# A decoder layer's down projection gets weight buffers of its own, and its weights are prepared three steps ahead

## The chip, the cores and the metric

The kernel runs on one core of one Trainium2 chip. Its time is the device time of one execution in microseconds. The engines of the core work side by side, each on its own queue of instructions, in order: PE (TensorE, matmuls and transposes), DVE (VectorE), ACT (ScalarE), POOL (GpSimd, here mainly a queue that issues DMAs) and SP (SyncE, a queue that issues DMAs). An instruction that waits for a semaphore holds everything behind it on its engine.

## The reference

One layer of a decoder, 512 tokens of width 2048, all in fp32: a modulation from c, an RMS norm, two attention mixers (one sparse with an indexer, one latent), a gated merge, and a feed-forward part with a causal convolution of width 3. The part around the change is the last line:

```python
h = rms_norm(x, g_ffn[l]) * (1.0 + sc_f) + sh_f
x = x + gt_f * conv_ffn(h, w_up[l], w_conv[l], b_conv[l], w_down[l])

def conv_ffn(h, w_up, w_conv, b_conv, w_down):
    u = h @ w_up                              # 2048 -> 2 * 5632
    conv = b_conv + sum(w_conv[j] * up[:, j:j + S] for j in range(3))   # up: u padded in front
    gate, val = split(conv)
    return (silu(gate) * val) @ w_down        # 5632 -> 2048
```

(Cut from the reference, with the loop over the convolution's taps written as a sum.)

## The kernel before, in words

**Precision.** fp32 products are made of three matmuls: each operand is split into a high part (`Copy` to fp32r on ACT) and a low part (the difference, on DVE), and high x high, high x low and low x high are accumulated (lines 1065 to 1067). So every weight tile costs one ACT and one DVE operation of its width before PE can use it; so does every activation tile (`split`, lines 113 to 115; the weights' halves are made by the same two lines).

**Seven products.** The gate, up and down projections go through `seven` (line 919). It multiplies a 2 x 2 block of weights with a 2 x 2 block of activations (the columns halved, 256 tokens each) in seven products of half-size blocks instead of eight. One `Pair` is a pair of 128-wide output columns, and has seven **steps**, in the order p1, p7, p6, p2, p5, p4, p3. Each step has a preparation (load blocks of weights, add or subtract them on DVE in `comb`, line 965, and make the halves in `hilo`), K x 3 matmuls of 256 columns, and an eviction from PSUM (e1, e7, e6 and e3 on ACT, line 969 or 971; e2, e5 and e4 on DVE, line 975 or 977). The first steps of a pair write one half of a bank pair each, and a later step of the same pair writes that bank again, so that it waits for the eviction of the step two before it.

**How far ahead.** The main loop (lines 1053 to 1070) prepares step q + 2 before it issues the matmuls of step q: AHEAD is 2. The weight buffers are five raw ones of 1104 columns, used in rotation through `rawq`, and three pairs of high and low (lines 81 to 91). All stages of the kernel use these. In most of the up projection some blocks lie in slots instead.

**The stages around the change.** The up projection is 40 pairs of K = 8 (280 steps, 24 matmuls and weight blocks of 1024 columns each). Each pair ends in a convolution, silu and product, and `f_out` writes the result f and the sums of it that the down projection needs to HBM, from POOL's queue. The down projection follows in the same list of steps: the 22 row pairs of f are cut in four **chunks** of `DH` = 6, 6, 5, 5, and each chunk goes over all eight pairs of output columns, 56 steps of K = 6 (18 matmuls, 768 columns) or K = 5 (15 matmuls, 640 columns). The results of the first three chunks are added to x1 in HBM by an accumulating DMA on POOL's queue (line 1526); the last chunk reads x1 back, adds it (line 1523) and writes the output.

**The activations of a chunk.** Each of the seven products of a chunk has its own operand, a "kind" of three tiles (two row pairs each, the last one half full where K = 5), which a chunk uses in all its eight pairs. `load_set` loads one kind of f from HBM into slots, on SP's queue, where the weight loads go too (line 1459). `split_set` splits a kind into high and low slots. `ahead` (line 1477) is called after each step; `left` is the number of steps until the chunk begins. It splits a whole kind every fourth step for four of the seven kinds, and one kind at every step from eight steps before the chunk on, as long as `2 * n + spare` slots are free. In the last seven steps of a chunk the kinds that are not needed any more are given back (line 1541).

**Slots.** 81 tiles of 128 x 512 fp32, handed out first in, first out (`get`, `put`). A slot that was given back may still be read by a DMA or an engine; who writes it next waits for that.

**Order.** The program is recorded in the order of the Python code, and a scheduler then orders each engine's instructions by priority and by its own estimate of times. So a split or a load may stand earlier on its engine than the code has it.

Of the kernel before, what the change touches and what calls it, by code (L numbers as in the profile page):

```python
# [10 lines left out]
F32 = mybir.dt.float32  # L11
# [20 lines left out]
def trunk_layer_kernel(  # L32
# [17 lines left out]
    PEU=((2, 5, 8, 11, 14),) * 2 + ((),) * 6,  # L50
    DH=(6, 6, 5, 5),
):
# [37 lines left out]

    rawq = deque(raw_b)

    def wtile(src, k0, kg, c0, n, pri=PRI, more=None):
        i = cnt["wt"] % NH
# [823 lines left out]

    def seven(work, pairs_of_banks, hook=None):
        def pair_steps(n, p):  # L920
# [34 lines left out]
            def hilo(t):  # L955
                i = cnt["wt"] % NH
# [15 lines left out]

            def plus(o, b, g, x):
                if g is not None:
                    V.scalar_tensor_tensor(o, b, g, x, op0=ALU.mult, op1=ALU.add)
                else:
                    V.tensor_tensor(o, b, x, ALU.add)  # L977

# [40 lines left out]
            def e1():  # L1019
                E["s"] = get()  # L1020
                copy(E["s"][:, :HT], X, g1)

            def e7():
                copy(E["s"][:, HT:], Y, g2)

            def e6():
                E["s6"] = get()
                copy(E["s6"][:, :HT], X, g2)

            def e2():  # L1030
                E["u1"] = get()
                plus(E["u1"][:, :HT], Z, g1, E["s"][:, :HT])

            def e5():
                E["u2"] = get()
                plus(E["u2"][:, HT:], X, g2, E["s"][:, HT:])
                put(E["s"])

            def e4():
                plus(E["u2"][:, :HT], Y, g2, E["s6"][:, :HT])  # L1040
                put(E["s6"])

# [7 lines left out]
        steps = [st + (p.K,) for n, p in enumerate(work) for st in pair_steps(n, p)]  # L1050
        AHEAD = 2
        ready = {}
        for q in range(len(steps) + AHEAD):
            if q < len(steps):
                ready[q] = steps[q][0]()
            if q < AHEAD:
                continue
            _, o, r, ev, first, K = steps[q - AHEAD]
            wh, wl = ready.pop(q - AHEAD)
            assert len(r) == K  # L1060
            for k in range(K):
                ks = slice(k * P, (k + 1) * P)
                rh, rl = r[k]
                last = k == K - 1
                PE.matmul(o, wh[:, ks], rh, start=first and k == 0, stop=False, skip_group_check=True)  # L1065
                PE.matmul(o, wh[:, ks], rl, start=False, stop=False, skip_group_check=True)  # L1066
                PE.matmul(o, wl[:, ks], rh, start=False, stop=last, skip_group_check=True)  # L1067
            ev()
            if hook:
                hook(q - AHEAD, len(steps))  # L1070

# [41 lines left out]
    seven([Pair(rs, lambda blk, i=i: w_gs[i, blk], gate_out(i)) for i in range((31 - G0) // 2)],  # L1113
          ((MM[0], MM[1]), (MM[2], MM[3])), gate_hook)
    for t in h[KH:] + [x for ts in h_sums for x in ts]:
        put(*t)
# [344 lines left out]

    def split_set():
        c, n, ts = coming.popleft()
        for i, t in enumerate(ts):
            hi, lo = getr(), getr()
            w = min(T, (DH[c] - 2 * i) * HT)
            split(hi[:, :w], lo[:, :w], t[:, :w])
            put(t)
            held_by[c][n] += [hi, lo]
            ops[c][n] += [(hi[:, o:o + HT], lo[:, o:o + HT]) for o in range(0, w, HT)]  # L1470

    def need(c):
        return (DH[c] + 1) // 2

    made = [0]

    def ahead(left, last):

        c = (coming or todo or [(9,)])[0][0]
        if c > last or left > 50:  # L1480
            return
        n, spare = need(c), 8 if c else 6
        if coming and coming[0][0] <= c and len(free) >= 2 * n + spare and (left <= 8 or left % 4 == 0 and made[0] < 4):
            made[0] = (made[0] + 1) % 7
            split_set()
        while todo and todo[0][0] <= c and len(coming) < (3 if c or len(free) > 15 else 1) and len(free) >= n + spare:
            load_set()


# [16 lines left out]
    work = [Pair(rs, lambda blk, i=i: w_ups[i, blk], ffn_out(i), slots=i < NF_ - 10) for i in range(NF_ - 4)]  # L1506
    n_up = len(work) * 7

# [23 lines left out]

    work += [down_pair(c, j) for c in range(len(DH)) for j in range(KD // 2)]

    def hook(q, n):
        if q < n_up:
            up_hook(q, n_up)
            return
        c, r = divmod(q - n_up, 56)
# [61 lines left out]
```

## Time and profile before

| | us |
|---|---|
| three runs, median | 2716.6 |
| lowest, highest | 2716.36, 2725.06 |
| profiled execution, as timed | 2718.77 |
| its span, first to last instruction | 2716.3 |
| mean granted TensorE clock | 0.99 |

All times of single instructions come from the profiled execution. The rows of windows give, for a stretch of the span, the time in which each engine was busy and the number of its instructions, then the granted TensorE clock, the mean busy share of the 16 DMA engines, and what they moved in GB/s. The rows of waits give who waited for whom: us in total, how often, the longest. In a row of a group stand line, engine, operation, what it writes and reads, count, busy time and mean duration in ns, then the idle time just before and what ended most of it. Names are those of the program without numbers: `raw`, `whi` and `wlo` are the weight buffers, `slot` a slot, `bank` a PSUM bank, `f` and `x` buffers in HBM, `in_w_down` the weights of the down projection.

The down projection's matmuls begin at about 2222 us of the span; the three changes of chunk are at about 2359, 2492 and 2608 us, and the last matmul ends at 2712 us.

### The profile page before, as it was taken

How to read it: one execution, taken by the hardware profiler on the slowest of the kernel's cores; microseconds unless marked ns; L12 is line 12 of the kernel's file. 1: busy time of each engine (PE TensorE's matmuls, PEld its weight loads, DVE VectorE, ACT ScalarE, POOL GpSimd, SP SyncE). 2: the span in 40 equal slices, each digit the busy share in tenths (PEclk: the TensorE clock that was granted, in tenths of full speed). 3: DMA queues.
4: the chain of work that ended last, by engine and by line, in shares of the span. 5: the costliest groups of instructions: out<-in, count | busy, mean ns of one | idle time of the engine just before them, and what ended most of it. 6: DMA issues, size and time to landing. Idle time of an engine off the chain costs nothing. (4 is left out here: it accounts for less than half of the span.)

```text
span 2716.3 us, 45517 instructions
## 1 busy us (share of the span) xinstructions
PE 2620.4 (96%) x17200; PEld 2351.7 (87%) x17200; DVE 2184.6 (80%) x3669; ACT 1285.3 (47%) x2069; POOL 270.5 (10%) x495
## 2 busy tenths in 40 slices
PE   6999999998999999999999999999999989898999
PEld 5777687778997767788789999999999989898989
DVE  7877966688878667983778989989889897777778
ACT  4333434334444455332545555555555464545554
POOL 1001011110032222110100000000000001011110
PEclk8999899999999999999999999999999999999999
DMA  9943136664585578962333333433433466766574
GB/s 343 341 153 98 34 110 213 197 214 156 190 269 164 161 255 288 323 238 93 132 114 124 134 137 113 147 120 114 148 120 128 140 205 154 187 141 173 137 206 125
DMA packets 236241, 464.33 MB, mean 171 GB/s; under 512 B 24331, under 2 KB 85413, under 8 KB 236021
## 3 DMA queue, kind: packets, MB, share of 16 engines
q1 hardware_dynamic: 199348, 368.79, 42.5%
q0 software_dynamic: 36640, 92.63, 11.7%
q8 instruction: 134, 2.20, 0.3%
q14 instruction: 87, 0.70, 0.1%
q10 hardware_dynamic: 32, 0.01, 0.0%
HBM read 397.11 MB, written 64.23 MB: 170 GB/s over the span
## 5 line engine op out<-in xcount | busy, mean ns | idle before, releaser
L1065 PE MATMUL bank<-slot,whi 128*128 128x256 f32 x3920 | 1109.9, 283 | 49.4 <-ACT slot L969 17.0
L1067 PE MATMUL bank<-slot,wlo 128*128 128x256 f32 x3920 | 1101.6, 282 | 8.3 <-DVE wlo L115 8.2
L1066 PE MATMUL bank<-slot,whi 128*128 128x256 f32 x3920 | 1104.4, 282 | 0.4 <-DVE slot L115 0.4
L1065 PEld LDWEIGHTS bank<-slot,whi 128*128 128x128 f32 x3920 | 743.4, 190 | 62.4 <-ACT slot L969 22.2
L1067 PEld LDWEIGHTS bank<-slot,wlo 128*128 128x128 f32 x3920 | 739.9, 189 | 10.8 <-DVE wlo L115 10.3
L1066 PEld LDWEIGHTS bank<-slot,whi 128*128 128x128 f32 x3920 | 741.7, 189 | 0.8 <-DVE slot L115 0.6
L114 ACT ACTIVATE whi<-raw 128x1024 fp32r<-128x1024 f32 (+2 forms) x458 | 424.6, 928 | 500.1 <-PE bank L1066 385.5
L115 DVE TENSOR_TENSOR wlo<-raw,whi 128x1024 fp32r<-128x1024 f32 (+2 forms) x458 | 482.1, 1056 | 61.7 <-ACT whi L114 59.6
L106 ACT ACTIVATE whi<-raw 128x1024 fp32r<-128x1024 f32 (+4 forms) x182 | 187.3, 1032 | 396.0 <-PE bank L120 201.8
L107 DVE TENSOR_TENSOR wlo<-raw,whi 128x1024 fp32r<-128x1024 f32 (+4 forms) x182 | 215.7, 1186 | 146.4 <-ACT whi L106 146.0
L965 DVE TENSOR_TENSOR raw<-raw,raw 128x1024 f32<-128x1024 f32 (+2 forms) x252 | 264.8, 1051 | 61.8 <-DMA raw<-in_w_down 33.3
L119 PE MATMUL bank<-wlo,slot 128*128 128x512 f32 (+2 forms) x768 | 297.4, 388 | 0.9 <-DVE wlo L107 0.9
L118 PE MATMUL bank<-whi,slot 128*128 128x512 f32 (+2 forms) x768 | 290.1, 391 | 4.7 <-ACT slot L385 4.3
L120 PE MATMUL bank<-whi,slot 128*128 128x512 f32 (+2 forms) x768 | 293.3, 385 | 0.0
L118 PE MATMUL bank<-slot,whi 128*128 128x512 f32 (+1 forms) x656 | 261.2, 405 | 3.3 <-ACT slot L1346 2.3
L119 PE MATMUL bank<-slot,whi 128*128 128x512 f32 (+1 forms) x656 | 263.1, 402 | 0.7 <-DVE slot L687 0.7
L120 PE MATMUL bank<-slot,wlo 128*128 128x512 f32 (+1 forms) x656 | 257.5, 401 | 0.0
L118 PEld LDWEIGHTS bank<-whi,slot 128*128 128x128 f32 x768 | 145.9, 190 | 36.1 <-ACT slot L385 4.3
L723 DVE SCALAR_TENSOR_TENSOR slot<-slot,c_act,slot 128x512 f32<-128x512 f32 x203 | 148.9, 745 | 33.9 <-DMA slot<-in_w_ada 32.8
L119 PEld LDWEIGHTS bank<-wlo,slot 128*128 128x128 f32 x768 | 146.2, 190 | 30.0 <-DVE wlo L107 1.4
L120 PEld LDWEIGHTS bank<-whi,slot 128*128 128x128 f32 x768 | 144.6, 188 | 29.0 <-issue 0.5
L114 ACT ACTIVATE whi<-slot 128x512 fp32r<-128x512 f32 x204 | 127.0, 630 | 79.4 <-PE bank L1066 63.8
(292 smaller groups left out, 3004.6 us busy)
## 6 DMA issues: line engine op xcount, KB each, us to landing
slot<-in_w_ada SPq DMA_DIRECT2D x344, 256.0 KB, 5.7
raw<-in_w_ups SPq DMA_DIRECT2D x126, 512.0 KB, 4.4
raw<-in_w_in SPq DMA_DIRECT2D x50, 512.0 KB, 3.6
raw<-in_w_down SPq DMA_DIRECT2D x64, 384.0 KB, 3.1
raw<-in_w_down SPq DMA_DIRECT2D x64, 320.0 KB, 3.4
slot<-f SPq DMA_DIRECT2D x154, 128.0 KB, 3.3
slot<-in_w_ups SPq DMA_DIRECT2D x68, 256.0 KB, 2.6
f<-slot POOLq DMA_DIRECT2D x66, 256.0 KB, 5.2
```

Source lines behind the costliest of these rows:

```text
L106: A.activation(hi, raw[:, :w], AF.Copy)
L107: V.tensor_tensor(lo, raw[:, :w], r32(hi), ALU.subtract)
L114: A.activation(dst_hi, src, AF.Copy)
L115: V.tensor_tensor(dst_lo, src, r32(dst_hi), ALU.subtract)
L118: PE.matmul(o, lh, rh, start=first, stop=False)
L119: PE.matmul(o, lh, rl, start=False, stop=False)
L120: PE.matmul(o, ll, rh, start=False, stop=last)
L723: V.scalar_tensor_tensor(acc, ts[i], c_act[:, k:k + 1], acc, op0=ALU.mult, op1=ALU.add)
L965: V.tensor_tensor(part(o, x, y), part(a, x, y), part(b, x, y), op)
L1065: PE.matmul(o, wh[:, ks], rh, start=first and k == 0, stop=False, skip_group_check=True)
L1066: PE.matmul(o, wh[:, ks], rl, start=False, stop=False, skip_group_check=True)
L1067: PE.matmul(o, wl[:, ks], rh, start=False, stop=last, skip_group_check=True)
```

## The change

- The weight buffers live in a pool of their own. When the last matmuls of the up projection have been issued in the code (`turn`), the pool is closed and opened anew at the same place, with seven raw buffers and four pairs of high and low, of 768 columns: 15 x 768 columns instead of 11 x 1104. A buffer of the new pool that overlaps one of the old pool waits for the old one's last use.
- `seven` returns two functions, `start` (the first AHEAD preparations) and `run`. The down projection is a list of its own with AHEAD = 3. The gate and up projections keep 2.
- The evictions add in place: e1 writes its half straight into `u1` and e7 and e6 into `u2`; e2, e5 and e4 add to them. The two helper slots of a pair are gone, and `u1` and `u2` are held from the first evictions on.
- The chunks are `DH` = 5, 6, 6, 5, and the packed weights follow.
- `split_tile` splits one tile instead of a kind, every third step from 54 steps before the chunk on, at every step from eight before, and a second one where the rest would not be done in time. It needs `2 + spare` free slots, and loading a kind needs its tiles and `spare`; `spare` is 12 (was 8) for all chunks but the first (6).

The diff, without the changes of the calls of `seven` for the gate projection, the packing and the renaming of `NH`:

```diff
-    NR, NH = 5, 3
-    WB = 1104
-    raw_b = [pool.tile([P, WB], F32, name=f"raw{i}") for i in range(NR)]
-    hi_b = [pool.tile([P, WB], F32R, name=f"whi{i}") for i in range(NH)]
-    lo_b = [pool.tile([P, WB], F32R, name=f"wlo{i}") for i in range(NH)]
+    wpool = ExitStack()
+    hi_b, lo_b, rawq = [], [], deque()
+    def weight_bufs(nr, nh, w):
+        wpool.close()
+        wp = wpool.enter_context(tc.tile_pool(name=f"w{w}", bufs=1))
+        rawq.clear()
+        rawq.extend([wp.tile([P, w], F32, name=f"raw{w}_{i}") for i in range(nr)])
+        hi_b[:] = [wp.tile([P, w], F32R, name=f"whi{w}_{i}") for i in range(nh)]
+        lo_b[:] = [wp.tile([P, w], F32R, name=f"wlo{w}_{i}") for i in range(nh)]
+    weight_bufs(5, 3, 1104)
...
-            def plus(o, b, g, x):
+            def plus(o, b, g):
                 if g is not None:
-                    V.scalar_tensor_tensor(o, b, g, x, op0=ALU.mult, op1=ALU.add)
+                    V.scalar_tensor_tensor(o, b, g, o, op0=ALU.mult, op1=ALU.add)
...
             def e1():
-                E["s"] = get()
-                copy(E["s"][:, :HT], X, g1)
+                E["u1"] = get()
+                copy(E["u1"][:, :HT], X, g1)
             def e7():
-                copy(E["s"][:, HT:], Y, g2)
+                E["u2"] = get()
+                copy(E["u2"][:, HT:], Y, g2)
             def e6():
-                E["s6"] = get()
-                copy(E["s6"][:, :HT], X, g2)
+                copy(E["u2"][:, :HT], X, g2)
             def e2():
-                E["u1"] = get()
-                plus(E["u1"][:, :HT], Z, g1, E["s"][:, :HT])
+                plus(E["u1"][:, :HT], Z, g1)
...
-        AHEAD = 2
-        for q in range(len(steps) + AHEAD):
+        def prepare(q):
             if q < len(steps):
                 ready[q] = steps[q][0]()
+        def start():
+            for q in range(AHEAD):
+                prepare(q)
+        def run(then=None):
+            for q, (_, o, r, ev, first, K) in enumerate(steps):
+                prepare(q + AHEAD)
...
+                if then and q == len(steps) - 1:
+                    then()
+                ev()
...
     def ahead(left, last):
         c = (coming or todo or [(9,)])[0][0]
-        if c > last or left > 50:
+        if c > last or left > 54:
             return
-        n, spare = need(c), 8 if c else 6
-        if coming and coming[0][0] <= c and len(free) >= 2 * n + spare and (left <= 8 or left % 4 == 0 and made[0] < 4):
-            made[0] = (made[0] + 1) % 7
-            split_set()
+        spare = 12 if c else 6
+        near = left <= 8
+        if coming and len(free) >= 2 + spare and (near or left % 3 == 0):
+            split_tile()
+            n = (DH[c] + 1) // 2
+            at = KINDS.index(coming[0][1]) if coming else 7
+            if any(len(coming[0][2]) + n * (i - at) > left + i - 2 for i in range(at, 7)):
+                split_tile()
...
-    work += [down_pair(c, j) for c in range(len(DH)) for j in range(KD // 2)]
+    up_start, up_run = seven(work, all_banks, up_hook)
+    work = [down_pair(c, j) for c in range(len(DH)) for j in range(KD // 2)]
     def hook(q, n):
...
-        ahead(0 if (coming or todo or [(0,)])[0][0] == c else 56 - r, c + 1)
-    seven(work, all_banks, hook)
+        ahead(-r if (coming or todo or [(0,)])[0][0] == c else 56 - r, c + 1)
+    down_start, down_run = seven(work, all_banks, hook, AHEAD=3)
+    def turn():
+        weight_bufs(7, 4, 768)
+        down_start()
+    up_start()
+    up_run(turn)
+    down_run()
```

More of the change, by code (lines that the diff above doesn't have):

```diff
@@ L1112, in trunk_layer_kernel @@
     rs = operands(h, h_sums)
-    seven([Pair(rs, lambda blk, i=i: w_gs[i, blk], gate_out(i)) for i in range((31 - G0) // 2)],
+    start, run = seven([Pair(rs, lambda blk, i=i: w_gs[i, blk], gate_out(i)) for i in range((31 - G0) // 2)],
           ((MM[0], MM[1]), (MM[2], MM[3])), gate_hook)
+    start()
+    run()
     for t in h[KH:] + [x for ts in h_sums for x in ts]:
@@ L1460, in load_set, with split_tile @@
         coming.append((c, n, ts))
[L1462 to L1475, printed above, removed]
+    def split_tile():
+        c, n, ts = coming[0]
+        t = ts.pop(0)
+        if not ts:
+            coming.popleft()
+        w = T if ts or DH[c] % 2 == 0 else HT
+        hi, lo = getr(), getr()
+        split(hi[:, :w], lo[:, :w], t[:, :w])
+        put(t)
+        held_by[c][n] += [hi, lo]
+        ops[c][n] += [(hi[:, o:o + HT], lo[:, o:o + HT]) for o in range(0, w, HT)]
     def ahead(left, last):
         c = (coming or todo or [(9,)])[0][0]
-        if c > last or left > 50:
+        if c > last or left > 54:
             return
-        n, spare = need(c), 8 if c else 6
-        if coming and coming[0][0] <= c and len(free) >= 2 * n + spare and (left <= 8 or left % 4 == 0 and made[0] < 4):
-            made[0] = (made[0] + 1) % 7
-            split_set()
-        while todo and todo[0][0] <= c and len(coming) < (3 if c or len(free) > 15 else 1) and len(free) >= n + spare:
+        spare = 12 if c else 6
[6 more added lines that the diff above has]
+                split_tile()
+        while todo and todo[0][0] <= c and len(coming) < (3 if c or len(free) > 15 else 1) \
+                and len(free) >= (DH[c] + 1) // 2 + spare:
             load_set()
@@ L1583 @@
             dn, k0, ds = a.reshape(DFF // (2 * P), 2, P, D), 0, []
[L1584 removed]
+            for n in (5, 6, 6, 5):
                 b = dn[k0:k0 + n].transpose(1, 0, 2, 3).reshape(2 * n * P, D)
```

53 lines of the change are left out of this document (21 added, 32 removed).

## The prediction

> **What bounds the kernel now.** I read the page first (span, busy time, slices), then the table of windows over the last third, then the waits of each engine there, then the durations by form, and last the order in which both programs' instructions stand.
>
> ```profile
> span 2716.3 us, 45517 instructions
> PE 2620.4 (96%) x17200; PEld 2351.7 (87%) x17200; DVE 2184.6 (80%) x3669; ACT 1285.3 (47%) x2069; POOL 270.5 (10%) x495
> PE   6999999998999999999999999999999989898999
> ```
>
> PE (TensorE) is busy 96% of the span. The change touches the up projection's end and the down projection, the last 16 slices; only there does PE fall back to 8. The windows show how much is lost (each engine: us busy, count; then clock, DMA share, GB/s):
>
> ```profile
> 1900.00:2200.00 300.00, 297.50 (x2501) 296.27 (x2500) 270.12 (x363) 164.65 (x244) 16.72 (x31) 1.00 0.41 134
> 2200.00:2260.00 60.00, 49.76 (x375) 47.89 (x374) 51.33 (x75) 35.44 (x59) 3.92 (x6) 0.94 0.78 237
> 2260.00:2305.00 45.00, 44.77 (x379) 44.56 (x378) 35.17 (x44) 21.86 (x33) 5.13 (x6) 1.00 0.59 141
> 2305.00:2390.00 85.00, 73.68 (x600) 71.34 (x599) 64.27 (x88) 45.93 (x75) 8.50 (x10) 1.00 0.67 171
> 2390.00:2440.00 50.00, 50.00 (x425) 50.00 (x424) 38.58 (x49) 24.74 (x37) 5.34 (x7) 1.00 0.59 143
> 2440.00:2520.00 80.00, 68.99 (x561) 66.85 (x560) 59.50 (x86) 42.76 (x74) 8.27 (x10) 1.00 0.67 170
> 2520.00:2565.00 45.00, 43.53 (x363) 42.95 (x362) 34.65 (x51) 22.91 (x38) 5.92 (x7) 1.00 0.60 139
> 2565.00:2625.00 60.00, 53.38 (x415) 51.09 (x415) 44.77 (x69) 30.08 (x54) 13.69 (x21) 0.97 0.73 196
> 2625.00:2705.00 80.00, 80.00 (x674) 79.82 (x674) 69.38 (x102) 42.86 (x73) 1.07 (x2) 1.00 0.50 152
> ```
>
> Undisturbed, 425 matmuls take 50.00 us: 0.1176 us each. At that pace a window's count gives the time it needed, and the rest is loss. The turn from up to down (2200 to 2260): 375 x 0.1176 = 44.1, loss 15.9. The three changes of chunk: 2305 to 2390 14.4, 2440 to 2520 14.0, 2565 to 2625 11.2, together 39.6. The chunks' middles and the last chunk: 0.4 + 0 + 2.3 + 0.7 = 3.4. In all **59 us** are to be had; the up projection before 2200 loses next to nothing. What PE waited for in the down stage, and what the engines in front of it waited for:
>
> ```profile
> PE bank L1065 <- ACT slot L969: 17.0, 18, 2.3
> PE bank L1065 <- DVE slot L975: 10.9, 13, 1.8
> PE bank L1067 <- DVE wlo L115: 4.8, 5, 1.8
> PE bank L1065 <- ACT whi L114: 3.9, 4, 1.9
> DVE raw L965 <- DMA raw<-in_w_down: 32.4, 33, 3.0
> DVE slot L115 <- DMA x<-slot: 16.7, 8, 3.0
> ACT slot L114 <- DMA x<-slot: 11.2, 7, 2.8
> SPq L1459 <- DMA x<-slot: 21.0, 5, 5.9
> DVE raw L965 <- DMA raw<-in_w_down: 3.8, 8, 0.7
> ```
>
> (The last row is 2623 to 2712 alone.) PE mostly waits for evictions, which stand in the in-order queues of ACT and DVE behind something that waits for a DMA: a weight block not landed (32.4 us on DVE), or a slot whose accumulate into x1 still reads it (16.7 on DVE, 11.2 on ACT). The last chunk has neither splits nor accumulates; its 3.8 us of weight waits cost PE 0.7.
>
> **The change part by part.** Nothing is removed or added in work: each engine's program has as many instructions as before, in sizes that only change places (chunk 0 has five row pairs, chunk 2 six). So all is waits and order. The evictions keep engine and shape and only add in place in u1 and u2; they cost 0, since what they read and write is of the same kind as before.
>
> ```profile
> L115 DVE TENSOR_TENSOR wlo<-raw,whi 128x768 fp32r<-128x768 f32 x111 | 104.9, 953 | 27.1 <-ACT whi L114 26.2
> L115 DVE TENSOR_TENSOR wlo<-raw,whi 128x640 fp32r<-128x640 f32 x112 | 91.4, 820 | 15.9 <-ACT whi L114 15.8
> L975 DVE SCALAR_TENSOR_TENSOR slot<-bank,mod,slot 128x256 f32<-128x256 f32 x96 | 45.9, 478 | 6.5 <-PE bank L1067 6.5
> L115 DVE TENSOR_TENSOR slot<-slot,slot 128x512 fp32r<-128x512 f32 x49 | 32.9, 685 | 9.9 <-DMA x<-slot 5.7 <-ACT slot L114 4.0
> L115 DVE TENSOR_TENSOR slot<-slot,slot 128x256 fp32r<-128x256 f32 x14 | 5.7, 421 | 15.4 <-DMA x<-slot 11.0 <-ACT slot L114 4.4
> L114 ACT ACTIVATE whi<-raw 128x768 fp32r<-128x768 f32 x111 | 93.6, 844 | 102.6 <-PE bank L1066 77.7 <-ACT slot L969 12.4 <-DVE raw L965 7.4
> L114 ACT ACTIVATE whi<-raw 128x640 fp32r<-128x640 f32 x112 | 82.2, 737 | 88.6 <-PE bank L1066 54.4 <-DVE raw L965 16.2 <-ACT slot L969 12.6
> raw<-in_w_down SPq DMA_DIRECT2D x64, 384.0 KB, 3.1
> raw<-in_w_down SPq DMA_DIRECT2D x64, 320.0 KB, 3.4
> x<-slot POOLq DMA_DIRECT2D x48, 256.0 KB, 4.8
> DMA to landing us min/median/max: 2.8/3.1/6.0
> ```
>
> *Seven raw buffers.* A step is 15 matmuls (1.76 us) with five row pairs, 18 (2.12 us) with six. In the old order the two tightest loads of a pair are freed 1.7 to 1.8 steps before their reader on DVE: 3.1 us or 3.7 us, against 3.4 or 3.1 to land. In the new order the tightest are 2.0 to 2.7 steps: 3.5 to 4.8, or 4.2 to 5.7. Most of the 28.6 us of weight waits that hurt (32.4 less 3.8) should go.
>
> *Four half pairs, three steps ahead.* A half pair still starts only when the step one buffer-round earlier ends, but PE now has three steps to do meanwhile: 5.3 us or 6.4 us, less 0.74 + 0.82 for the two halves (0.84 + 0.95 for six), so 3.7 or 4.6 us of lateness are covered, where two steps covered 2.0 or 2.4. The longest waits above are 3.0: this cover alone swallows a late low half. An eviction has only the cover it had, one step.
>
> *Splits a tile at a time, spare 12, two slots fewer per pair.* The new order still bunches them. In the last pair of chunk 0 DVE has 11 x 0.82 + 3 x 0.478 + 10 x 0.685 = 17.3 us for 105 matmuls (12.3 us); in the first of chunk 1, 11 x 0.953 + 1.4 + 7 x 0.685 = 16.7 us for 14.8. That is 6.9 too much, of which 3.7 is covered: 3 us lost, a new cost of a five-pair chunk beside a six-pair one. At the next change it is 8 splits and then 6 with 3 short ones: 34.7 for 29.6, 5.1 over, 4.6 covered. At the third DVE is inside the cover. And the slots are not old: 6 splits still come under two steps behind the accumulate whose slot they take (7 before). But on ACT, where a wait holds evictions, only one of the six is left.
>
> *What it moves onto SP.* A load of f waits at the head of SP's queue for its slot, and the weight loads wait behind it. Old order: 5 loads behind the accumulate of the pair just done, just the 5 waits of 21.0 us above. New order: 15. At 4.2 us each SP stands still 63 us. Bounds per event on PE: 0, if cover and longer reserve take it, and 4.2, if nothing does; I take 0.5 us, nearer to nothing, because 4.2 less the reserve (0 to 1 us beyond landing) is inside the 3.7 to 4.6. So 7 us, put with the chunk changes.
>
> *The turn.* Before, three loads of w_down went out at 2211, and up's last high half stood on ACT behind splits that waited for f; from 2213 to 2218 PE ran 7 matmuls where 42 fit:
>
> ```profile
> 2211.02 1.38 SPq L952 DMA_DIRECT2D raw<-in_w_down  x3
> 2213.97 1.67 ACT L114 ACTIVATE slot<-slot 128x512 fp32r<-128x512 f32 x3 [1.97 <-DMA slot<-f]
> 2217.03 0.84 ACT L114 ACTIVATE whi<-raw 128x768 fp32r<-128x768 f32 x1 [1.39 <-DMA raw<-in_w_down]
> 2213.00:2218.00 5.00, 0.76 (x7) 0.55 (x6) 4.14 (x7) 2.64 (x5) 0.00 (x0) 1.00 0.90 302
> 2218.00:2222.00 4.00, 4.00 (x22) 4.00 (x23) 3.36 (x5) 0.40 (x1) 0.00 (x0) 0.61 0.87 268
> ```
>
> Now the new pool lies where the old one lay: in the new order the first load of w_down **waits for up's last matmul**, with everything behind it. Behind that wait on SP: the other five weight loads and the f loads of chunk 1. From that matmul on: first load 3.1 us, second half a microsecond later (1.38 / 3), 3.6. Then DVE in its order, up to the low half of the third step: five combinations and five low halves at 0.82, two 512-wide operations of the last up pair and three splits at 0.685, two short ones at 0.42: 12.5 us, so 16.1. By then PE can have done 49 matmuls, 5.8 us: 10.3 lost. With a slow clock for a while (+1.4, below) and the next pair's catching up (+2.3) I put the turn at 14 (15.9 before). Bounds: 9 (DVE's operations overlap a little, nothing else), 22 (first landing at the 6.0 maximum, +2.9, two more slow stretches, +2.8, and as much again in the next pair).
>
> The last row's clock: after the stall it was 0.61 for 4 us, 22 matmuls where 34 fit; 12 x 0.1176 = 1.4 us extra, which the turn of 14 has in it. [...]
>
> *Sum.* Turn 14. Chunk changes: 3 + 1 + 0 of DVE load, 7 of SP, and 7 of the slot waits with an eviction behind them (a quarter of 16.7 + 11.2, between none and the half that a cover of one step would leave): 18. Middles and last chunk 6: the 3.4 of now and as much for the splits that move there. That is 38 of the 59: **21 us gained**. The earlier stages keep their order but for a few neighbours; I count 0 for them, ±3. The profiled execution took 2718.8 (span 2716.3 and 2.5 around it), so 2697.8 there; the median of the three runs is 2716.6, 2.2 lower, so **2696**.
>
> **The rivals.**
> *More than that.* Three steps cover every wait (longest 3.0) and the turn is at its floor: 9 + 6 + 3 = 18 lost, 41 gained, 2676. For it: the last chunk lost 0.7 with weight waits present. Against: DVE's overload at the first change.
> *The turn eats it.* The turn at 22, the chunk changes at 24 because the reserve makes the slots no older, middles 6: 52, gain 7, 2710. For it: DMA is at 0.87 to 0.90 around the turn and six loads go at once. It decides when the first load lands at 6 rather than 3.
> *SP becomes the bound (slower).* Place: f loads at the head of SP, 15 times. Price: if each costs PE its 4.2 us, 63 + turn 14 + 2 = 79 against 59: 20 us slower, 2737. It decides from (59 + 8 - 16) / 15 = 3.4 us of PE per event on. For it: the rule "one queue for both loads" is unchanged and the held loads tripled; against: old events of 4.2 us stood with only two steps of cover, and all chunk changes together lost 39.6.
>
> **How the numbers follow.** Forecast 0.60 (2683 to 2708), more 0.12, the turn eats it 0.15, SP 0.13. About 0.3%, 8 us, is what a measurement can tell from no change: faster 0.72, same 0.15, slower 0.13. The range leaves out SP and the outer half of "more": 2681 to 2715, which holds the turn's bounds (-5, +8).
>
> **What would show it.** Right: waits of DVE for in_w_down well under half of 32.4; the window around the turn with a gap of 4 to 6 us between the last up and first down matmul, then DVE without a pause for 12 us; chunk changes each losing under 9; SP's waits for x near 60. Wrong: the turn above 22; PE waiting for low halves (wlo) more than for evictions; a loss in the chunk middles above 10; a shift before 2200.

## The result, and the profile after

The changed kernel is **slower**: 2735.5 us median of 8 runs (2727.9 to 2743.5) against 2716.8 us (2715.5 to 2725.1) for the kernel before on the same chip. The ratio is 1.0059, with a 95% interval of 1.0041 to 1.0078. The forecast was 2696, with a range that ended at 2715. The profiled execution took 2735.9 us, with a span of 2734.2.

The page of the changed kernel, span and TensorE's slices:

```profile
span 2734.2 us, 45439 instructions
PE 2628.8 (96%) x17200; PEld 2360.8 (86%) x17200; DVE 2183.6 (80%) x3669; ACT 1282.7 (47%) x2069; POOL 271.4 (10%) x495
PE   6999999999999999999999999999999989798999
```

DVE, ACT and POOL are as busy as before, to 3 us. PE is busy 8.4 us longer with the same 17200 matmuls, at a mean granted clock of 0.986 for 0.990. So the added time is waiting again, and matmuls at a lower clock behind the waits; the last 16 slices have a 7 that was not there. The table of windows over the last third (us busy and count of each engine, then clock, DMA share, GB/s), cut at the turn, at the three changes of chunk and at the middles:

```profile
1900.00:2195.00 295.00, 289.80 (x2436) 287.83 (x2435) 263.72 (x357) 158.73 (x234) 16.75 (x31) 1.00 0.39 131
2195.00:2255.00 60.00, 48.36 (x362) 46.22 (x361) 50.41 (x77) 36.68 (x63) 3.91 (x6) 0.91 0.73 218
2255.00:2325.00 70.00, 65.87 (x545) 64.84 (x544) 51.02 (x75) 35.39 (x60) 8.54 (x10) 1.00 0.63 154
2325.00:2385.00 60.00, 45.55 (x335) 43.78 (x335) 42.23 (x58) 29.14 (x49) 5.11 (x6) 0.91 0.63 168
2385.00:2460.00 75.00, 72.68 (x606) 72.07 (x605) 57.26 (x74) 36.64 (x56) 8.55 (x10) 1.00 0.60 145
2460.00:2525.00 65.00, 55.04 (x421) 53.20 (x419) 46.73 (x66) 33.78 (x58) 5.13 (x6) 0.95 0.65 178
2525.00:2600.00 75.00, 73.70 (x597) 72.88 (x598) 54.71 (x69) 34.82 (x54) 9.09 (x11) 0.98 0.59 137
2600.00:2640.00 40.00, 34.76 (x283) 33.74 (x282) 28.88 (x43) 19.62 (x34) 11.69 (x19) 1.00 0.81 237
2640.00:2725.00 85.00, 85.00 (x715) 85.00 (x714) 73.07 (x108) 44.15 (x75) 0.00 (x0) 1.00 0.39 131
```

At the pace of 0.1176 us a matmul, each window less its count times 0.1176 is its loss, as in the prediction:

| part | before | forecast | after | how |
|---|---|---|---|---|
| turn | 15.9 | 14 | 17.4 | 60 - 362 x 0.1176 |
| change 0 to 1 | 14.4 | | 20.6 | 60 - 335 x 0.1176 |
| change 1 to 2 | 14.0 | | 15.5 | 65 - 421 x 0.1176 |
| change 2 to 3 | 11.2 | | 6.7 | 40 - 283 x 0.1176 |
| all changes | 39.6 | 18 | 42.8 | |
| middles, last chunk | 3.4 | 6 | 15.3 | 5.9 + 3.7 + 4.8 + 0.9 |
| sum | 59 | 38 | 75.5 | |

The first row is new in this reading: 300 us of up lost 5.9 us before (300 less 2501 x 0.1176), and 295 us lose 8.5 now. What PE and the engines in front of it waited for, from the turn to the end (us, times, longest):

```profile
PE bank L1074 <- ACT slot L977: 18.1, 13, 4.0
PE bank L1074 <- ACT whi L122: 15.3, 9, 6.0
PE bank L1074 <- DVE slot L983: 12.4, 10, 2.9
DVE raw L973 <- DMA raw<-in_w_down: 51.3, 29, 5.3
ACT slot L122 <- DMA slot<-f: 31.7, 17, 3.9
SPq L1474 <- DMA x<-slot: 68.3, 15, 9.8
```

SP's 15 waits for x are there as foretold (63 foretold). But the waits for weights did not go: they rose from 33.3 to 51.3 us (32.4 in the prediction's slightly shorter window), and ACT waits for f 31.7 us, where it was 7.8.

The worst place is the change from chunk 0 to 1. Its rows from the timeline (start, length, engine, operation, and in brackets the wait ahead of it): SP's queue, then DVE and ACT.

```profile
2346.54 12.38 SPq L1474 DMA_DIRECT2D slot<-f  x18
2359.02 0.38 SPq L960 DMA_DIRECT2D raw<-in_w_down  x1
2359.44 0.90 SPq L1474 DMA_DIRECT2D slot<-f  x2
2360.44 13.02 SPq L960 DMA_DIRECT2D raw<-in_w_down  x4
2367.11 1.95 DVE L973 TENSOR_TENSOR raw<-raw,raw 128x768 f32<-128x768 f32 x2 [5.14 <-DMA raw<-in_w_down]
2369.15 1.58 ACT L122 ACTIVATE whi<-raw 128x768 fp32r<-128x768 f32 x2 [9.07 <-DVE raw L973]
```

And two windows there:

```profile
2365.00:2370.00 5.00, 2.14 (x19) 1.94 (x17) 1.92 (x2) 0.85 (x2) 0.00 (x0) 0.94 0.03 12
2370.00:2376.00 6.00, 4.86 (x22) 4.86 (x23) 3.57 (x5) 3.01 (x5) 0.00 (x0) 0.50 0.44 119
```

Eighteen loads of f occupy SP's queue for 12.4 us with no weight load between them. Then DVE stands 5.1 us for a weight, ACT 9.1 us for DVE, PE runs dry for 4.0 us, and from 2370 to 2376 its clock is 0.50: 22 matmuls where 51 fit, 29 x 0.1176 = 3.4 us on top, of which PE stood idle for 1.1 (6.00 less 4.86). This chain looked like the whole story, and it is why the first experiments went for SP. They showed that SP's queue is the smaller part.

### The profile page after: what moved, and what is told of

It reads as the page before. It is cut to its first block, busy times and chain, and to the rows that moved or that the text cites. A ratio compares the mean times of both kernels' runs of the same rounds, so it can differ in the third digit from the quotient of the medians.

```text
span 2734.2 us, 45439 instructions
## 1 busy us (share of the span) xinstructions
PE 2628.8 (96%) x17200; PEld 2360.8 (86%) x17200; DVE 2183.6 (80%) x3669; ACT 1282.7 (47%) x2069; POOL 271.4 (10%) x495
## 5 line engine op out<-in xcount | busy, mean ns | idle before, releaser
L973 DVE TENSOR_TENSOR raw<-raw,raw 128x1024 f32<-128x1024 f32 (+2 forms) x252 | 264.7, 1052 | 74.6 <-DMA raw<-in_w_down 51.3
L128 PEld LDWEIGHTS bank<-whi,slot 128*128 128x128 f32 x768 | 145.1, 189 | 28.6 <-issue 0.3
```

Of the source, the lines that this page charges most:

```text
L128: PE.matmul(o, ll, rh, start=False, stop=last)
L973: V.tensor_tensor(part(o, x, y), part(a, x, y), part(b, x, y), op)
```

## The experiments

All times are against the kernel before on the same chip; the ratio stands with its 95% interval. Ratios differ from the quotient of the medians by up to 0.2%, so "us" below is the ratio less 1, times 2716.6, good to about 4 us.

| run | what differs | median | ratio | us |
|---|---|---|---|---|
| after | the change | 2735.5 | 1.0059 (1.0041 to 1.0078) | +16.0 |
| e1 | after, f loads on POOL | 2724.8 | 1.0034 (1.0022 to 1.0046) | +9.2 |
| e2 | after, slots of u put back two pairs later | 2725.2 | 1.0037 (1.0021 to 1.0053) | +10.1 |
| e3 | after, order 6, 6, 5, 5 | 2726.7 | 1.0049 (1.0033 to 1.0065) | +13.3 |
| e4 | before, f loads on POOL | 2709.4 | 0.9977 (0.9964 to 0.9989) | -6.2 |
| e5 | before, evictions in place, closed pool | 2737.5 | 1.0088 (1.0059 to 1.0116) | +23.9 |
| e6 | e5 and the new buffers | 2724.0 | 1.0023 (1.0009 to 1.0038) | +6.2 |
| e7 | e3, f loads on POOL | 2722.4 | 1.0020 (1.0008 to 1.0032) | +5.4 |
| e8 | e6, f loads on POOL | 2724.4 | 1.0028 (1.0018 to 1.0038) | +7.6 |
| e9 | before, evictions in place | 2737.9 | 1.0072 (1.0053 to 1.0091) | +19.6 |
| e10 | after, nothing closed at the turn | 2729.5 | 1.0046 (1.0032 to 1.0061) | +12.5 |
| e11 | after, old evictions | 2719.5 | 1.0002 (0.9992 to 1.0011) | +0.5 |
| e12 | before, in place in down alone | 2725.6 | 1.0028 (1.0012 to 1.0043) | +7.6 |
| e13 | before, in place in gate and up alone | 2724.1 | 1.0025 (1.0010 to 1.0040) | +6.8 |
| e14 | e11, f loads on POOL | 2724.6 | 1.0029 (1.0015 to 1.0043) | +7.9 |
| e15 | e14, order 6, 6, 5, 5, nothing closed | 2717.4 | 1.0005 (0.9988 to 1.0022) | +1.4 |
| e16 | e6, old evictions | 2715.3 | 0.9995 (0.9983 to 1.0006) | -1.4 |
| e17 | e16, nothing closed | 2713.6 | 0.9985 (0.9975 to 0.9995) | -4.1 |
| e18 | after, old evictions and order 6, 6, 5, 5 | 2701.5 | 0.9939 (0.9918 to 0.9961) | -16.6 |

**SP's queue: e1, e2, e4.** The theory was rival three of the prediction: loads of f held at the head of SP. In e1 and e4 the load goes to POOL's queue:

```diff
-            SP.dma_start(ts[-1][:, (i % 2) * HT:(i % 2 + 1) * HT], f_d[base[c] + i][m][:, o * HT:(o + 1) * HT])
+            G.dma_start(ts[-1][:, (i % 2) * HT:(i % 2 + 1) * HT], f_d[base[c] + i][m][:, o * HT:(o + 1) * HT])
```

> The changed kernel with the loads of f (line 1474) issued from POOL's queue instead of SP's; nothing else. Theory SP (f loads stand at the head of SP's queue until an accumulate has read its slot, and the weight loads behind them come late): SP's waits for x (68.3 us, 15) go to nearly 0, DVE's waits for in_w_down (51.3 us) fall below 15, and of the 77 us that PE loses around and in the down projection 20 or more go: 2735 becomes 2705 to 2715. Rival SLOTS (the slots themselves come free too late, whatever queue holds the load): weight waits fall, but ACT's waits for f (24.5 us) grow by as much, and the time stays within 6 us of 2735. Rivals TURN and ORDER (the emptied turn; the five-pair chunk in front): within 6 us of 2735 and c0 to c1 still loses near 18.

In e2 the slots wait in a queue of their own, so that a load meets none that is still read:

```diff
-            put(*us, *x1)
+            if x1:
+                put(*us, *x1)
+            else:
+                aged.append(us)
+                if len(aged) > 2:
+                    put(*aged.popleft())
...
-        spare = 12 if c else 6
+        spare = 12 - 2 * len(aged) if c else 6
```

> The changed kernel with the two slots of a finished pair put back two pairs later (four slots withheld, the reserve lowered from 12 to 8, so that loads and splits come at the same steps). A load of f then finds slots whose accumulate is long done, but stays in SP's queue. Theory SP: SP's waits for x fall from 68.3 us to under 25, weight waits from 51 to under 25, time 2705 to 2718. Rival SLOTS: also faster, and by more than with the loads on POOL, since ACT's and DVE's waits for x (10.3 and 4.5 us) go too. Rivals TURN and ORDER: within 6 us of 2735.

> The kernel before with its loads of f issued from POOL's queue. Theory SP: SP's waits for x (21.0 us, 5) go, and as they were a third as many, the gain is a third of that in the changed kernel: 3 to 10 us faster than 2716.6. Rivals: no difference (within 3 us), or some us slower if loads that are put behind accumulates on POOL's queue come late themselves.

Each of e1 and e2 takes 6 to 7 us off the changed kernel by the ratios, 10 by the medians; their intervals overlap that of the changed kernel, so the size is uncertain. e2 leaves SP 46.9 us of waits for x, more than expected. The waits of e1, DVE's and POOL's from the turn on:

```profile
DVE raw L973 <- DMA raw<-in_w_down: 52.5, 34, 5.0
POOL slot L1474 <- DMA x<-slot: 53.3, 16, 7.2
```

SP no longer waits for x at all, yet DVE waits for weights as long as ever, 52.5 us. So the loads of f in front of the weights were not what made the weight waits, and by this run each of the 15 events cost PE about 6.8 / 15 = 0.45 us (0.7 by the medians). The kernel before gains as much from the same edit (6.2 us) with 5 events. Theory SP, as the cause of the loss, falls.

**The order of the chunks: e3.** The default is set back, and the weights are packed to match:

```diff
-    DH=(5, 6, 6, 5),
+    DH=(6, 6, 5, 5),
...
-            for n in (5, 6, 6, 5):
+            for n in (6, 6, 5, 5):
```

> The changed kernel with the chunks in the old order, 6, 6, 5, 5 row pairs. Rival ORDER (eleven splits and low halves in the five-pair pair before a six-pair chunk overload DVE): c0 to c1, which loses 18, falls to under 10, time 2720 to 2727. Theory SP: the f loads stand behind as many accumulates, SP's waits for x stay near 68 us, the time stays within 6 us of 2735. Rival TURN: within 4 us of 2735, since the turn is unchanged but for steps of 18 matmuls instead of 15.

By the medians it is 8.8 us faster, by the ratios 2.7, with intervals that overlap: unclear in time. Its trace and e18 say more (below).

**A ladder from before to after: e5 to e8.** In e5 the changed kernel has the old split rule, the old order, two steps and a turn that opens the old sizes again:

```diff
-        weight_bufs(7, 4, 768)
+        weight_bufs(5, 3, 1104)
...
-    down_start, down_run = seven(work, all_banks, hook, AHEAD=3)
+    down_start, down_run = seven(work, all_banks, hook, AHEAD=2)
```

> The changed kernel with all undone but the turn and the evictions in place: the weight buffers are closed and opened again at their old sizes (five raw, three high and low of 1104 columns), two steps ahead, the old rule for splits, the old order 6, 6, 5, 5. So it is the kernel before plus the closed buffers at the turn. Theory TURN (the first load of w_down now waits for up's last matmul and PE runs dry): 5 to 10 us slower than before's 2716.4, 2721 to 2726, and PE's loss around the turn grows from 14 to about 20. Theory SP: within 3 us of before, SP's waits for x 15 to 35 us.

e6 takes these two lines back, so that it has the new buffers and three steps; e7 and e8 are e3 and e6 with the line of e1.

> The same with the new buffers and three steps ahead as well (seven raw, four high and low of 768 columns), still the old rule for splits and the old order 6, 6, 5, 5. My prediction's buffers (more cover for late weights): 5 to 10 us faster than the turn alone. Theory SP (the longer run-ahead lets SP come to the loads of f before the slots are free): SP's waits for x grow to 45 us or more though the rule for loads is that of before, and the time is 0 to 5 us slower than the turn alone.

> The changed kernel with both edits that each took 9 to 10 us off: loads of f on POOL's queue and the chunks in the order 6, 6, 5, 5. If SP and ORDER are two causes (a load of f held in front of the weights; DVE with 94 us of work for a chunk of 100 us of matmuls), they add: 2715 to 2718. If they are two ways to take the same stall away (the change from chunk 0 to 1, where PE's clock falls after a gap), most of the second is lost: 2722 to 2726.

> The new buffers three steps ahead with the old rule for splits and the old order, and the loads of f on POOL's queue. If the new rule for splits costs something, this is faster than the same with the new splits (6655, f on POOL); if it brings something, slower; beyond 3 us either way it counts. Theory SP: 5 to 10 us faster than the buffers alone. With TURN (5 to 10 us) still in it: 2710 to 2720.

e5 was the surprise: +24 us, where 5 to 10 were expected for a closed pool. The new buffers then gain 18; the new splits (e6 to e3) cost 7 and the order 3, both with intervals that overlap. With f on POOL, e7 is 8 us below e3 and e8 no different from e6: once more no fixed price of SP's waits.

**The evictions in place: e9, e11, e12, e13, and the turn, e10.** e5 holds two edits. e9 puts the in-place evictions alone into the kernel before, e11 takes them alone out of the changed kernel:

```diff
             def e7():
-                copy(E["s"][:, HT:], Y, g2)
+                E["u2"] = get()
+                copy(E["u2"][:, HT:], Y, g2)
...
             def e5():
-                E["u2"] = get()
-                plus(E["u2"][:, HT:], X, g2, E["s"][:, HT:])
-                put(E["s"])
+                plus(E["u2"][:, HT:], X, g2)
```

> The kernel before with one part of the change: the evictions add in place in u1 and u2. The turn alone (with these evictions) was 20 us slower than before, where 5 to 10 were expected; this splits the 20. Rival EVICT (in place, a slot is taken four steps earlier for u2, and in the up projection a weight block that is loaded into a slot comes later): 5 to 12 us slower than before, 2722 to 2729, PE's loss in the first 39 pairs of up at 19 to 23 instead of 14. Theory TURN (the closed buffers carry all of it): within 3 us of 2717, as my prediction had it when it put the evictions at 0.

> The changed kernel with the evictions of before (three slots, s, s6 and u1, u2 taken late). EVICT: 5 to 12 us faster than 2735, with PE's loss in the first 39 pairs of up back from 19 to about 14. TURN, SP, ORDER: within 4 us of 2735; two slots more per pair in the down projection may cost 1 to 3.

Both came out as EVICT has it, and above its range: +19.6 us in the kernel before, 15.5 us off in the changed one. The same edit is measured twice more: 7.6 us between e16 and e6, and 29.9 between e18 and e3. All four pairs have intervals that don't meet. The closed pool, e5 less e9, is left with 4 us, inside the error. e10 asks the turn directly; the buffers are cuts of tiles that stay open:

```diff
+    back = [pool.tile([P, n * 1104], d, name=f"w{t}") for t, n, d in (("raw", 5, F32), ("whi", 3, F32R), ("wlo", 3, F32R))]
...
-        wpool.close()
-        wp = wpool.enter_context(tc.tile_pool(name=f"w{w}", bufs=1))
...
-        rawq.extend([wp.tile([P, w], F32, name=f"raw{w}_{i}") for i in range(nr)])
+        rawq.extend([back[0][:, i * w:(i + 1) * w] for i in range(nr)])
```

> The changed kernel with the weight buffers of both layouts as cuts of three tiles that stay open: seven raw lie where the five lay, four high and four low where the three lay. Nothing is closed at the turn, so the first load of w_down waits only for up's last use of the raw buffer that lies there (DVE), and no longer for up's last matmul. Theory TURN: the gap of 6.3 us at the turn goes to under 2, and the time falls by 8 to 20 us, 2715 to 2727. Rivals SP, ORDER, EVICT: the loads that come earlier at the turn only wait elsewhere, within 4 us of 2735.

PE's gap there, in front of the first matmul of down, was 6.02 us in the changed kernel; here the longest wait at the turn is 1.82. The first of the two rows is e10's:

```profile
2226.94 0.38 PE L1071 MATMUL bank<-slot,wwhi 128*128 128x256 f32 x1 [1.82 <-ACT wwhi L119]
2195.00:2255.00 60.00, 52.16 (x386) 50.24 (x385) 52.18 (x78) 35.87 (x62) 3.13 (x6) 0.91 0.71 222
```

The window loses 60 - 386 x 0.1176 = 14.6 us, 2.8 less than the 17.4, but up ends 6 us later in it. Counted by the starts of the matmuls, from 168 before the end of up to 168 after it, the loss is 17.7 us in the changed kernel and 13.8 in e10: 3.9 less, about what the gap got shorter. In time it is 3.5 us, within the error. The rest of the turn's loss is there without the gap too.

e12 and e13 split the evictions by stage: each body of e1 to e4 asks whether the pair has a scale (down) or not (gate, up), and takes the new form on one side and the old one on the other.

> The kernel before with evictions in place in the down projection alone (pairs with a scale); gate and up as before. The whole edit cost 19 us; this and the next run split it. Theory SLOTS (with two slots instead of four taken per pair the freed slots of u come to the loads of f and the splits sooner after their accumulate: SP's waits for x went from 21.0 us, 5, to 39.6, 14): 8 to 15 us slower than before, SP's waits for x near 40. Rival UP-ORDER (the cost sits in the up projection, where 13 evictions instead of 1 stand on DVE right behind two combinations that wait for a weight): within 3 us of before.

> The kernel before with evictions in place in gate and up alone; the down projection as before. UP-ORDER: 4 to 12 us slower than before, PE's loss in the first 39 pairs of up 18 or more instead of 14.4. SLOTS: within 5 us of before. If both runs are slower the two add up to the 19 us.

Both are slower, 7.6 and 6.8 us, so both theories hold for their stage (e12 just under its range); together they make 14.4 of the 19.6 us of e9, which is inside the error. In e12, from the turn on, first SP and then DVE:

```profile
SPq L1479 <- DMA x<-slot: 38.6, 14, 5.0
DVE raw L965 <- DMA raw<-in_w_down: 50.3, 34, 5.0
```

And in e13, where down has the old evictions:

```profile
SPq L1479 <- DMA x<-slot: 19.9, 5, 5.6
DVE raw L965 <- DMA raw<-in_w_down: 28.7, 29, 3.1
```

The edit alone, with the old buffers, the old reserve and the old split rule, takes SP's waits from 5 to 14 and the weight waits from 33.3 to 50.3. It takes two slots from the free list per pair in place of four, and u2 three steps earlier; other operations then meet the slots that an accumulate still reads. In up, here are DVE's wait for a weight that a combination into a slot needs, and PE's wait for evictions, 1420 to 2190, first before, then e13:

```profile
DVE slot L965 <- DMA raw<-in_w_ups: 36.1, 26, 3.6
PE bank L1065 <- DVE slot L977: 2.9, 7, 1.0
```

```profile
DVE slot L965 <- DMA raw<-in_w_ups: 53.4, 31, 3.6
PE bank L1085 <- DVE slot L977: 6.0, 16, 0.7
```

In DVE's order, 13 or 14 evictions of up stand right behind both combinations of that kind when they are in place (13 in the changed kernel, 14 in e13), and 1 when they are not. So an eviction now waits behind a weight load. PE's loss in the first 39 pairs of up (the time of 6552 matmuls less 6552 x 0.1176) is 17.1 us before and 22.0 in e13. One profile alone would not show this: e12, with the old evictions there, loses 21.2. Over all twenty profiles it holds, 20.5 to 27.3 us (mean 23.7) in the eleven kernels with evictions in place in up, and 14.6 to 21.2 (mean 17.5) in the nine without: about 6 us.

**What adds and what does not: e14 to e18.**

> The changed kernel with the old evictions and, besides, the loads of f on POOL's queue. With the old evictions SP still waits for x 62 us. Theory SP: as in the changed kernel, 8 to 11 us off 2719.5: 2709 to 2712. If the price of an SP wait hangs on the evictions in place: within 4 us of 2719.5.

> A version for speed: the new buffers, three steps ahead and the new rule for splits kept; evictions of before, the order 6, 6, 5, 5, the loads of f on POOL's queue, and the weight buffers cut from three open tiles so that nothing is closed at the turn. If the four causes add: 2735 less 16 (evictions), 9 (order), 6 (turn), 4 to 10 (SP), so 2694 to 2700. If they are ways of taking the same stalls away twice: 2705 to 2712, no better than the kernel before with f on POOL (2709).

> The kernel before with the new buffers alone: seven raw, four high and low, three steps ahead, the pool closed and opened at the turn; evictions, splits and order of before. With the evictions in place this form took 2724.0, and they cost 16 to 19. If the parts add: 2705 to 2709, 7 to 12 us faster than before, the first form with new buffers that gains. If the gain of the buffers (13.5 us) was only the return of what the evictions had cost: within 4 us of 2717.

> The same with the weight buffers cut from three open tiles, so that the first load of w_down no longer waits for up's last matmul. In the changed kernel this took 6 us off: 4 to 8 us faster than the same with the closed pool if it adds; within 3 us if what starts earlier waits elsewhere.

> The changed kernel with the evictions of before and the order 6, 6, 5, 5 (it keeps the new buffers, the closed pool and the new splits). If evictions (16) and order (9) add: 2708 to 2712. The new splits cost 2.7 with the evictions in place: if that holds, 2 to 4 us slower than the buffers alone with old evictions.

e14 and e15 missed: with the old evictions, f on POOL makes the changed kernel 7 us slower, and all four "good parts" together bring nothing. Their traces say where: f on POOL moves splits into chunk 0. From e11 to e14 DVE has 150 operations in chunk 0 (from its first matmul to the first of chunk 1) where it had 140, and PE loses 27.4 us there where it lost 21.7; from e18 to e15 (which also leaves the pool open) 154 where it had 140, and 29.7 us where it lost 10.3. That is as much as e15's whole span is longer than e18's (2716.2 against 2697.2). The operations added are splits, 13 of the 14 in e15. e16 answers the question of the buffers: without the evictions, they gain nothing by themselves (-1.4); their 18 us in e6 were mostly the return of what the evictions had cost. e17 is 2.7 us below it, again too little to tell. e18, the changed kernel with only the evictions and the order set back, is **faster than both kernels**, and than either expectation: 0.9939, 0.9918 to 0.9961, from 4 runs. Its windows, cut in the same way:

```profile
2195.00:2250.00 55.00, 45.30 (x348) 43.42 (x347) 49.19 (x69) 34.26 (x56) 3.91 (x6) 0.94 0.82 249
2250.00:2320.00 70.00, 69.67 (x582) 69.06 (x581) 55.47 (x73) 36.20 (x56) 8.40 (x10) 1.00 0.57 139
2320.00:2380.00 60.00, 55.52 (x451) 53.80 (x450) 48.62 (x67) 33.30 (x56) 5.25 (x7) 1.00 0.76 211
2380.00:2440.00 60.00, 59.59 (x498) 58.98 (x497) 46.11 (x59) 30.66 (x48) 6.85 (x8) 1.00 0.60 149
2440.00:2520.00 80.00, 74.00 (x590) 72.02 (x589) 62.06 (x92) 42.12 (x75) 8.55 (x10) 0.98 0.65 166
2520.00:2560.00 40.00, 38.95 (x321) 38.29 (x321) 31.25 (x48) 22.50 (x39) 5.11 (x6) 1.00 0.64 151
2560.00:2610.00 50.00, 45.29 (x368) 43.95 (x367) 39.10 (x60) 26.13 (x47) 13.38 (x21) 1.00 0.76 214
2610.00:2690.00 80.00, 79.73 (x668) 79.33 (x667) 66.30 (x99) 40.26 (x68) 0.54 (x1) 1.00 0.40 136
```

Turn 14.1, changes 7.0 + 10.6 + 6.7 = 24.3, middles and last chunk 1.6 + 1.4 + 2.3 + 1.4 = 6.7: 45.1 in all, where the forecast had 14 + 18 + 6 = 38 and the kernel before 59. Against e11, which differs by the order alone, it is 17 us faster, with intervals that don't meet. Cut as the changed kernel, e11 loses 13.3 at the turn, 10.7 + 10.9 + 5.1 = 26.7 at the changes and 11.4 + 7.5 + 4.7 + 0.9 = 24.5 in the middles and the last chunk. So the order gains 18 us in the middles, most of them in chunks 0 and 1, whose two rows in e11 are

```profile
2255.00:2325.00 70.00, 63.35 (x498) 62.32 (x497) 50.40 (x75) 32.92 (x57) 8.39 (x10) 0.95 0.61 148
2385.00:2460.00 75.00, 71.24 (x574) 70.02 (x575) 55.39 (x71) 35.37 (x56) 7.66 (x9) 0.98 0.55 136
```

The other pairs that differ by the order alone agree. Chunks 0 and 1 together lose 51.5 us in the changed kernel and 27.6 in e3, 42.8 in e11 and 18.9 in e18, 45.9 in e1 and 29.4 in e7. And over the 336 matmuls around the change from chunk 0 to 1, PE loses 10.4 to 21.7 us in the six kernels with 5, 6, 6, 5, and 3.5 to 11.5 in the fourteen with 6, 6, 5, 5. The times of e3 and e7 show less: from e1 to e7 the turn and the later chunks give 13 us back, and up begins 6 us later in e3's profile than in the changed kernel's, though no edit between them touches what comes before. A likely reason is DVE's load in chunk 0 as a whole. First the changed kernel, then e18:

```profile
2224.80:2346.80 122.00, 107.39 (x842) 104.02 (x843) 94.12 (x140) 64.69 (x111) 13.61 (x17) 0.97 0.66 171
```

```profile
2220.00:2349.00 129.00, 125.38 (x1010) 122.77 (x1011) 106.67 (x140) 68.79 (x108) 13.61 (x17) 0.98 0.66 177
```

With five row pairs DVE has 94.1 us of work for 842 x 0.1176 = 99.0 us of matmuls, 95%; with six it has 106.7 for 118.8, 90%. e11 is like the changed kernel, 93.3 us for 98.8. A chunk of five in front of one of six does the splits of the large chunk in the time of the small one, and has half the room to catch up after any wait. That the load is the cause is argued from these shares; no run changed it alone.

## Why the prediction was wrong

- **The step that failed** is "The evictions keep engine and shape and only add in place in u1 and u2; they cost 0". The instruction count and the durations were right (480 ns an eviction on DVE, 478 before). But the edit takes fewer slots, at other steps, from a first-in first-out list, and that moved the order on DVE in up and put 9 more waits on SP in down. It measured 7.6 to 29.9 us, 15.5 in the changed kernel itself, which is why the kernel got slower and not merely no faster. An edit with no work of its own was priced by its work.
- **The order of chunks** was priced at "3 us lost, a new cost of a five-pair chunk beside a six-pair one", plus 1. This term was the second to fail, and is why no gain was left: with the old evictions it measured 17 us; in the changed kernel as it is, 3 to 9 in time, which can't be told from nothing, and 24 on the traces of chunks 0 and 1. The load of DVE was worked out for the last pair and the first; the whole chunk at 95% was not looked at. One of the prediction's own signs of being wrong came with it, a loss in the middles above 10: it is 15.3.
- From the forecast to the result are 39.5 us. By the medians the evictions make 16.0 of them (the changed kernel to e11), the order 18.0 (e11 to e18) and the rest 5.5. e18, with these two set back, has a turn of 14.1 against 14 and middles of 6.7 against 6; its changes are 24.3 against 18, of which the forecast had 4 for the five-pair chunk that e18 does not have in front. So the total of e18 is near the forecast partly by luck.
- **The turn** was right in size: 17.4 in the changed kernel, between the bounds 9 and 22. The wait of the first load for up's last matmul is real (that matmul ends at 2218.77, the load goes out at 2218.80, and PE has 6.0 us of gap), and leaving the buffers open took about 4 us of it away. After the gap the clock was 0.50 to 0.76 from 2225 to 2231; in e18, where PE was busy for 0.03 us from 2213 to 2220, it was 0.50 from 2220 to 2224. In the changed kernel a gap of 2.9 us in front of 2340.2 left it at 1.00, and one of 4.0 us, from 2367.1 to 2371.1, brought it to 0.50. Shorter waits were followed by 0.50 too. In the changed kernel there were two of 2.9 and 2.0 us, from 2351 to 2358 with some 2.5 us of matmuls between them, and the clock was 0.50 from 2359.7 to 2362 (a mean of 0.74 over 2360 to 2365). In the kernel before, one of 2.0 us ended at 2224.7, close behind a stretch at 0.61 (2218 to 2222), and the clock was 0.50 from 2226 to 2229. So in these traces the length of the last gap alone does not tell the clock behind it: 2.9 us once left it at 1.00, and 2.0 us twice came ahead of 0.50.
- **SP's price** per event was put at 0.5 us; e1 gives 0.45 to 0.7, but the same edit gave anything from a gain of 8 us to a loss of 7 in other kernels, so the agreement is partly luck. The rival "SP becomes the bound" named 2737, and the time is 2735.5, but not for its reason: with all those waits gone the kernel stays 9 us slower than before, and e18 has 14 of them and is the fastest.
- **"Most of the 28.6 us of weight waits that hurt should go"** was wrong as a sign to look for: they are 51.3 us in the changed kernel and 45.9 in e18, which gained. The lead of 4.2 to 5.7 us for 768 columns was set against 3.1 us to land, and in the changed kernel they took a median of 4.8. That DVE, three steps ahead, also comes to a load earlier and waits longer without PE noticing fits e18, but was not tested. What PE itself waits for tells the cases apart: 45.8 us for the three rows of the changed kernel above, 36.0 for the same three before (17.0, 10.9 and 8.1 from the turn on), 33.8 in e11, and 20.9 in e18:

```profile
PE bank L1078 <- DVE slot L983: 9.2, 12, 2.6
PE bank L1078 <- ACT whi L122: 8.1, 4, 7.2
PE bank L1078 <- ACT slot L977: 3.6, 8, 1.0
```

What stays open: the prices do not add. The new splits cost 7 us with the evictions in place (e6 to e3) and gain 15 without (e16 to e18); f on POOL takes 6 to 8 us off three kernels (e1, e4, e7), does nothing in one (e8) and costs 7 in another (e14). Each edit gives the engines a new order in the whole last third, and which waits then meet is not settled by a sum. For f on POOL the traces give one part: it takes SP's holds away, and puts 7 to 13 more operations of DVE into chunk 0, in all five pairs that differ by it alone. Nor was it tried whether the number of slots taken or the step at which u2 is taken puts the combinations ahead of the evictions.

## What to carry to other kernels

An edit that leaves every instruction as it is but takes buffers from a shared list at another step is not free (7.6 to 29.9 us here): compare the order on each engine before and after, in every stage that shares the code, and price the places where something that waits for a transfer now stands ahead of something that another engine waits for. Undo the parts of a change that seem to do nothing, too: here two of them hid a gain of 0.6%. A long wait in a trace is a suspect and no verdict; taking the waits of 68 us on SP away moved the time by 7.

## What the runs showed of the hardware

Landing times differed between the kernels: the 384 KB weight blocks took a median of 3.1 us before, 4.8 in the changed kernel and 3.8 in e18, the rows of the page for the changed kernel and for e18 being

```profile
raw<-in_w_down SPq DMA_DIRECT2D x64, 384.0 KB, 4.8
```

```profile
raw<-in_w_down SPq DMA_DIRECT2D x64, 384.0 KB, 3.8
```

These blocks belong to chunks 1 and 2 in the changed kernel and to 0 and 1 in e18, so part of it may be the place; that was not separated.
